# Gate projections of the RG-LRU: one block-diagonal 128x128 product, or four 64x64 products in quarters of the array

## The chip, the cores and the metric

One core of a Trainium2 chip runs the whole program. The metric is the device time of one execution in microseconds, as a median over timed runs. A profiled execution of the same program gives the trace from which all rows below are taken.

## The reference, cut to what matters

Two layers of a decoder trunk run over 2048 tokens of width 1024. The even layer holds retention and stick-breaking attention, the odd layer an HGRN2 recurrence and an RG-LRU. The change touches the gates of the RG-LRU, where each of 8 blocks of 64 channels has its own 64x64 weight for the recurrence gate `r` and for the input gate `ig`:

```
xb = x.reshape(B, S, LRU_BLOCKS, LRU_BW)          # 8 blocks of 64 channels
r  = sigmoid(einsum('bsni,nij->bsnj', xb, w_a).reshape(B, S, W) + b_a)
ig = sigmoid(einsum('bsni,nij->bsnj', xb, w_x).reshape(B, S, W) + b_x)
log_a = -8 * r * softplus(-lam);  a = exp(log_a)
u = sqrt(-expm1(2 * log_a)) * ig * x
h_t = a_t * h_(t-1) + u_t
```

## The kernel before, in words

Everything is float32. Each layer is done in two halves of 1024 tokens, each half in groups `g` of 512 tokens. Activations lie with channels on partitions, so a projection (`proj`, L153) is a stream of 24 products of 128x128 by 128x512 that add into one bank of PSUM, tag `pp`. Its weights and inputs are split in a high and a low part, hence three products for each of 8 blocks of input channels.

The odd layer's half is `hgrn`. It first runs the input projections of HGRN head 0 and of the first 128 channels of the RG-LRU, then weaves the chunk scan of head h (`head_scan`, L829 to L913) with the projections of head h+1 and of RG-LRU channels j = h+1. The scan's products go to PSUM banks of tag `z`, of which there are two; the L880 and L872 products are steps of it. L872 already uses parts of the array: outputs of 32 or 64 partitions, with all 128 input rows.

`lx_proj(j)` handles channels j*128 to j*128+127, two blocks of the RG-LRU. When its two groups are projected, VectorE makes the convolution `xc` (L725 to L727), and `gates(0)` and `gates(1)` are put off through `later` by estimated amounts of TensorE time (L750, L751). A call of `gates(g)` does two float32 products, one for `r` and one for `ig`, each with a block-diagonal 128x128 weight `bd` (L733), and after each product one Sigmoid on ScalarE out of the `z` bank (L734). `gates(1)` goes on with Exp, Tanh and Sqrt (L738 to L740), which need other activation tables than one another in part, and with the scan over time on VectorE (L747), whose result `lg_proj` uses much later. There are 2 halves x 4 j x 2 g = 16 calls.

`bd` is cleared on VectorE (L707) and then filled by four DMAs on the SP queue (L710). The biases `bga` and `bgx` are small constants loaded once by `odd_const` (L701, L702).

The tile framework fixes the order of instructions on each engine when the program is built. It goes by its own estimates of durations: a product that would wait for a bank or an operand by that estimate lets later ready work pass it. A bank of a tag is given to its next user when the last reader of the last user is through.

Of the kernel before, what the change touches and what calls it, by code (L numbers as in the profile page):

```python
# [9 lines left out]
F32 = mybir.dt.float32  # L10
F32R = mybir.dt.float32r
U8 = mybir.dt.uint8
AF = mybir.ActivationFunctionType
# [18 lines left out]
def tile_trunk(ctx: ExitStack, tc: tile.TileContext, a: dict, out: bass.AP):  # L32
    nc = tc.nc
# [4 lines left out]
    const = ctx.enter_context(tc.tile_pool(name="const", bufs=1))  # L38
# [9 lines left out]
    def bank(tag):  # L48
        return (o_bank[-1] if tag == "o" else ps_p).tile([128, 512], F32, tag=tag, name=tag)
# [110 lines left out]
    def later(ns, fn):  # L160
        late.append([ns, fn])
# [47 lines left out]
    def mix_store(half, e, g, t, eng=nc.sync):  # L209
        eng.dma_start(out=mixd[half][g][:, e, :], in_=t)  # L210
# [443 lines left out]
    lam8 = const.tile([128, 4], F32, name="lam8")  # L654
    cw = const.tile([128, 4, 4], F32, name="cw")
    cb = const.tile([128, 4], F32, name="cb")
    bga = const.tile([128, 4], F32, name="bga")
    bgx = const.tile([128, 4], F32, name="bgx")

    def odd_const():  # L660
        with tc.tile_pool(name="oc", bufs=1) as p:
            def ld(name, ap):
                t = p.tile([128, 4], F32, tag=name, name=name)
                nc.sync.dma_start(out=t, in_=ap.rearrange("(j p) -> p j", p=128))
                return t

            lg = ld("lg", a["hgrn_lb_logits"][0])
            t = p.tile([128, 4], F32, name="t")
            e = p.tile([128, 4], F32, name="e")
            nc.vector.tensor_tensor(out=t, in0=lg, in1=lg, op=ALU.subtract)  # L670
            nc.scalar.activation(out=e, in_=t, func=AF.Exp)
            nc.vector.reciprocal(out=t, in_=e)
            nc.vector.tensor_tensor(out=e, in0=e, in1=t, op=ALU.mult)
            nc.vector.tensor_tensor(out=lb, in0=e, in1=e, op=ALU.subtract)
            nc.vector.tensor_scalar(out=olb, in0=lb, scalar1=-1.0, scalar2=1.0, op0=ALU.mult, op1=ALU.add)
            lm = ld("lm", a["lru_lambda"][0])
            ng = p.tile([128, 4], F32, name="ng")
            nc.vector.tensor_scalar(out=ng, in0=lm, scalar1=-1.0, scalar2=None, op0=ALU.mult)
            ab = p.tile([128, 4], F32, name="ab")
            nc.vector.tensor_tensor(out=ab, in0=ng, in1=lm, op=ALU.max)  # L680
            w = p.tile([128, 4], F32, name="w")
            nc.scalar.activation(out=w, in_=ab, func=AF.Exp, scale=-1.0)
            d = p.tile([128, 4], F32, name="d")
            nc.vector.tensor_scalar(out=d, in0=w, scalar1=2.0, scalar2=None, op0=ALU.add)
            nc.vector.reciprocal(out=d, in_=d)
            nc.vector.tensor_tensor(out=w, in0=w, in1=d, op=ALU.mult)
            w2 = p.tile([128, 4], F32, name="w2")
            nc.vector.tensor_tensor(out=w2, in0=w, in1=w, op=ALU.mult)
            s = p.tile([128, 4], F32, name="s")
            nc.vector.memset(s, 1.0 / 19.0)  # L690
            for m in range(17, 0, -2):
                nc.vector.tensor_tensor(out=s, in0=s, in1=w2, op=ALU.mult)
                nc.vector.tensor_scalar(out=s, in0=s, scalar1=1.0 / m, scalar2=None, op0=ALU.add)
            nc.vector.tensor_tensor(out=s, in0=s, in1=w, op=ALU.mult)
            nc.vector.tensor_scalar(out=ng, in0=ng, scalar1=0.0, scalar2=None, op0=ALU.max)
            nc.vector.scalar_tensor_tensor(out=s, in0=s, scalar=2.0, in1=ng, op0=ALU.mult, op1=ALU.add)
            nc.vector.tensor_scalar(out=lam4, in0=s, scalar1=4.0, scalar2=None, op0=ALU.mult)
            nc.vector.tensor_scalar(out=lam8, in0=s, scalar1=-8.0, scalar2=None, op0=ALU.mult)
            nc.sync.dma_start(out=cw, in_=a["conv_w"][0].rearrange("k (j p) -> p k j", p=128))
            nc.sync.dma_start(out=cb, in_=a["conv_b"][0].rearrange("(j p) -> p j", p=128))  # L700
            nc.sync.dma_start(out=bga, in_=a["lru_b_a"][0].rearrange("(j p) -> p j", p=128))  # L701
            nc.sync.dma_start(out=bgx, in_=a["lru_b_x"][0].rearrange("(j p) -> p j", p=128))  # L702

    def lru(half, xT, p1, p5, gt_p, sg_p, M):
        p = p1
        bd = p1.tile([128, 4, 2, 128], F32, name="bd")
        nc.vector.memset(bd, 0.0)  # L707
        for i, nm in enumerate(("lru_w_a", "lru_w_x")):
            for b in range(2):
                nc.sync.dma_start(out=bd[64 * b:64 * b + 64, :, i, 64 * b:64 * b + 64],  # L710
                                  in_=a[nm][0].rearrange("(j b) i o -> b i j o", b=2)[b])
        HT = {}

        def lx_proj(j):
            new = lambda tag: p.tile([128, 1024], F32, tag=tag, name=tag)
            lx = p.tile([128, 1028], F32, tag="lx", name="lx")

            def use_x(g, ps):
                nc.scalar.copy(out=lx[:, 3 + g * 512:515 + g * 512], in_=ps)
                if g == 0:  # L720
                    nc.gpsimd.tensor_copy(out=lx[:, 0:3], in_=lru_x[:, j, :])
                    return
                nc.gpsimd.tensor_copy(out=lru_x[:, j, :], in_=lx[:, 1024:1027])
                xc, r, ig = new("xc"), new("r"), new("ig")
                nc.vector.tensor_scalar(out=xc, in0=lx[:, 0:1024], scalar1=cw[:, 0, j:j + 1], scalar2=cb[:, j:j + 1], op0=ALU.mult, op1=ALU.add)  # L725
                for k in range(1, 4):
                    nc.vector.scalar_tensor_tensor(out=xc, in0=lx[:, k:k + 1024], scalar=cw[:, k, j:j + 1], in1=xc, op0=ALU.mult, op1=ALU.add)  # L727

                def gates(g):
                    c = slice(g * 512, g * 512 + 512)  # L730
                    for i, (t, bias) in enumerate(((r, bga), (ig, bgx))):
                        gp = bank("z")
                        nc.tensor.matmul(gp, bd[:, j, i, :], xc[:, c], start=True, stop=True)  # L733
                        nc.scalar.activation(out=t[:, c], in_=gp, func=AF.Sigmoid, bias=bias[:, j:j + 1])  # L734
                    if g == 0:
                        return
                    av = lx[:, 0:1024]
                    nc.scalar.activation(out=av, in_=r, func=AF.Exp, scale=lam8[:, j:j + 1])  # L738
                    nc.scalar.activation(out=r, in_=r, func=AF.Tanh, scale=lam4[:, j:j + 1])
                    nc.scalar.activation(out=r, in_=r, func=AF.Sqrt)  # L740
                    nc.gpsimd.tensor_tensor(out=ig, in0=ig, in1=xc, op=ALU.mult)
                    nc.vector.scalar_tensor_tensor(out=r, in0=av, scalar=1.0, in1=r, op0=ALU.add, op1=ALU.mult)
                    if half == 0:
                        nc.vector.memset(r[:, 0:1], 1.0)
                    nc.vector.tensor_tensor(out=ig, in0=ig, in1=r, op=ALU.mult)
                    ht = p5.tile([128, 1024], F32, tag="ht", name="ht")
                    nc.vector.tensor_tensor_scan(out=ht, data0=av, data1=ig, initial=lru_h[:, j:j + 1], op0=ALU.mult, op1=ALU.add)  # L747
                    nc.gpsimd.tensor_copy(out=lru_h[:, j:j + 1], in_=ht[:, 1023:1024])
                    HT[j] = ht
                later(6000, lambda: gates(0))  # L750
                later(8000, lambda: gates(1))  # L751

            yield from proj(1, 2048 + j * 128, xT, use_x)

        def lg_proj(j):
            def use_g(g, ps):
                if j == 3 and g == 1:
                    for tt in range(EARLY[1]):
                        mix_rows(half, M, tt, wr_p, "raw")
                gt = gt_p.tile([128, 512], F32, tag="gt", name="gt")  # L760
                silu_to(gt, ps, sg_p)
                last = j == 3
                (nc.vector if last else nc.gpsimd).tensor_tensor(out=gt, in0=gt, in1=HT[j][:, g * 512:g * 512 + 512], op=ALU.mult)
                if last:
                    mix_direct(M, g, gt)
                else:
                    mix_store(half, 4 + j, g, gt)

            yield from proj(1, 2560 + j * 128, xT, use_g)

        return lx_proj, lg_proj
# [225 lines left out]
```

## Time and profile before

| What | Value |
|---|---|
| Time, median of 3 runs | 2305.8 us (2302.98 to 2307.48) |
| Profiled execution, its own time | 2313.08 us |
| Its span, first to last instruction | 2311.2 us |
| TensorE busy | 2233.0 us, 97% of the span |
| VectorE, ScalarE, GpSimd busy | 61%, 48%, 30% |
| Granted TensorE clock, mean | 0.996 of full speed |

The profiled execution lies 7.3 us above the median of the timed runs. TensorE shows two rows: PE for products and PEld for weight loads, which overlap. A float32 product shows as two MATMUL instructions, so 32 gate products are 64 MATMUL rows. A row of the timeline merges instructions that follow without a gap: start, length, engine, line, operation, tiles, shapes, count.

### The profile page before, as it was taken

How to read it: one execution, taken by the hardware profiler on the slowest of the kernel's cores; microseconds unless marked ns; L12 is line 12 of the kernel's file. 1: busy time of each engine (PE TensorE's matmuls, PEld its weight loads, DVE VectorE, ACT ScalarE, POOL GpSimd, SP SyncE). 2: the span in 40 equal slices, each digit the busy share in tenths (PEclk: the TensorE clock that was granted, in tenths of full speed). 3: DMA queues.
4: the chain of work that ended last, by engine and by line, in shares of the span. 5: the costliest groups of instructions: out<-in, count | busy, mean ns of one | idle time of the engine just before them, and what ended most of it. 6: DMA issues, size and time to landing. Idle time of an engine off the chain costs nothing.

```text
span 2311.2 us, 34986 instructions
## 1 busy us (share of the span) xinstructions
PE 2233.0 (97%) x12928; PEld 1886.8 (82%) x12928; DVE 1398.7 (61%) x2113; ACT 1107.5 (48%) x2306; POOL 696.6 (30%) x988
## 2 busy tenths in 40 slices
PE   7999999999999999999899999999999999999998
PEld 6888787789888888787777997878878977878788
DVE  4554666673677776878788454655555535455543
ACT  5443445553466666777666433244245323433431
POOL 0432334410055444555653001222230013122400
PEclk9999999999999999999999999999999999999999
DMA  6333333254622231322223541111126411111161
GB/s 193 110 105 108 106 117 105 92 157 141 209 81 76 82 90 53 94 60 87 81 60 114 184 164 37 42 44 35 49 76 206 163 46 33 46 33 41 64 206 74
DMA packets 244139, 223.11 MB, mean 97 GB/s; under 512 B 21376, under 2 KB 197888, under 8 KB 243968
## 3 DMA queue, kind: packets, MB, share of 16 engines
q1 hardware_dynamic: 243808, 220.35, 31.0%
q8 instruction: 102, 1.67, 0.3%
q14 instruction: 69, 0.57, 0.1%
q0 software_dynamic: 160, 0.52, 0.1%
HBM read 147.43 MB, written 52.43 MB: 86 GB/s over the span
## 4 chain that ended last, share of the span: by engine, by line
PE 76%; DVE 10%; DMA 4%; ACT 4%; issue 3%; POOL 2%; SPq 0%; DVEq 0%; POOLq 0%; ACTq 0%
PE pp L153 42%; PE o L515 4%; PE z L626 4%; PE tr L500 4%; PE pp L626 4%; PE o L626 4%; DVE a L487 2%; PE z L474 2%; PE z L473 2%; DMA mr<-mixd 2%; PE z L880 2%; PE z L733 1%; DVE wtl L505 1%; DVE xc L727 1%; PE tr L113 1%
## 5 line engine op out<-in xcount | busy, mean ns | idle before, releaser
L153 PE MATMUL pp<-xh,wh 128*128 128x512 f32 x1664 | 688.9, 414 | 6.8 <-DVE rst L357 6.2
L153 PE MATMUL pp<-xh,wl 128*128 128x512 f32 x1664 | 658.4, 396 | 2.3 <-DVE wl L133 2.3
L153 PE MATMUL pp<-xl,wh 128*128 128x512 f32 x1664 | 655.8, 394 | 0.0
L153 PEld LDWEIGHTS pp<-xh,wl 128*128 128x128 f32 x1664 | 313.3, 188 | 71.7 <-DVE wl L133 3.5
L490 POOL TENSOR_TENSOR b<-b,a 128x511 f32<-128x511 f32 (+2 forms) x320 | 315.7, 987 | 181.8 <-DVE a L487 109.2
L153 PEld LDWEIGHTS pp<-xh,wh 128*128 128x128 f32 x1664 | 314.5, 189 | 60.3 <-issue 3.0
L153 PEld LDWEIGHTS pp<-xl,wh 128*128 128x128 f32 x1664 | 315.1, 189 | 48.7 <-issue 0.5
L487 DVE TENSOR_TENSOR_SCAN a<-a,past 128x512 f32<-128x512 f32 x192 | 244.4, 1274 | 75.1 <-ACT a L477 74.3
L477 ACT ACTIVATE a<-z 128x512 f32<-128x512 f32 (+2 forms) x320 | 172.2, 538 | 235.6 <-PE z L474 193.5
L133 DVE TENSOR_TENSOR wl<-raw,wh 128x1024 fp32r<-128x1024 f32 x136 | 170.9, 1257 | 128.9 <-ACT wh L132 128.9
L132 ACT CAST wh<-raw 128x1024 fp32r<-128x1024 f32 x136 | 142.9, 1052 | 186.0 <-PE pp L153 159.8
L505 DVE TENSOR_TENSOR wtl<-tr,wth 128x512 fp32r<-128x512 f32 (+1 forms) x320 | 190.3, 596 | 46.5 <-ACT wth L504 45.5
L72 POOL TENSOR_TENSOR rs<-rs,mhalf 128x1 f32<-128x1 f32 (+1 forms) x96 | 67.0, 698 | 479.0 <-DVE rs L71 468.4
L504 ACT CAST wth<-tr 128x512 fp32r<-128x512 f32 (+1 forms) x320 | 169.8, 531 | 72.2 <-PE tr L500 70.6
L500 PE MATMUL tr<-ident,b 128*128 128x128 f32 x1088 | 175.9, 276 | 10.6 <-DVE wtl L505 9.8
L500 PEld LDWEIGHTS tr<-ident,b 128*128 128x128 f32 x1088 | 133.8, 141 | 58.3 <-DVE wtl L505 17.1
L478 ACT ACTIVATE b<-z 128x512 f32<-128x512 f32 (+2 forms) x320 | 171.1, 535 | 0.1
L482 DVE TENSOR_TENSOR_SCAN a<-a,past 128x128 f32<-128x128 f32 (+3 forms) x128 | 104.3, 816 | 91.2 <-ACT a L477 90.6
L515 PE MATMUL o<-wth,v 128*128 128x512 f32 (+1 forms) x320 | 126.8, 396 | 1.1 <-ACT mol L521 1.1
L852 POOL TENSOR_TENSOR kg<-kg,t 128x256 f32<-128x256 f32 x96 | 71.3, 743 | 172.9 <-PE z L880 107.6
L480 POOL TENSOR_SCALAR_AFFINE_SELECT b<-b 128x128 f32<-128x128 f32 x128 | 42.3, 330 | 261.9 <-ACT b L478 223.6
L473 PE MATMUL z<-k,qh 128*128 128x512 f32 (+2 forms) x320 | 119.3, 373 | 1.1 <-DMA qh<-qrh 0.9
(216 smaller groups left out, 4196.7 us busy)
## 6 DMA issues: line engine op xcount, KB each, us to landing
raw<-in_even_w_in SPq DMA_DIRECT2D x56, 512.0 KB, 3.9
raw<-in_odd_w_in SPq DMA_DIRECT2D x48, 512.0 KB, 3.7
xr<-in_x SPq DMA_DIRECT2D x32, 512.0 KB, 5.4
xr<-x1d SPq DMA_DIRECT2D x32, 512.0 KB, 5.3
mr<-mixd SPq DMA_DIRECT2D x32, 448.0 KB, 4.8
qh<-qrh SPq DMA_DIRECT2D x64, 128.0 KB, 2.3
ql<-qrl SPq DMA_DIRECT2D x64, 128.0 KB, 2.4
x1d<-y SPq DMA_DIRECT2D x16, 512.0 KB, 3.5
```

Source lines behind the costliest of these rows:

```text
L133: nc.vector.tensor_tensor(out=wl, in0=raw, in1=wh.bitcast(F32), op=ALU.subtract)
L153: nc.tensor.matmul(ps, w[:, k, :], xx[g][:, k, :], start=(n == 0), stop=(n == 3 * KD - 1))
L473: nc.tensor.matmul(z[:, 0:n], qh[:, tcol], K[e, c][:, 0:n], start=True, stop=False)
L477: nc.scalar.activation(out=A[:, 0:n], in_=z[:, 0:n], func=AF.Sigmoid, scale=-0.125)
L478: nc.scalar.activation(out=B[:, 0:n], in_=z[:, 0:n], func=AF.Sigmoid, scale=0.125)
L487: nc.vector.tensor_tensor_scan(out=A[:, ::-1], data0=A[:, ::-1], data1=past[:, 0:1].to_broadcast([128, 512]), initial=carry[ti][:, 0:1], o ...
L490: nc.gpsimd.tensor_tensor(out=B[:, 0:n - 1], in0=B[:, 0:n - 1], in1=A[:, 1:n], op=ALU.mult)
L500: nc.tensor.transpose(tr[:, ti * 128:ti * 128 + 128], bt[ti][:, sj * 128:sj * 128 + 128], ident)
L504: nc.scalar.copy(out=wh[:, cols], in_=tr[:, cols])
L505: nc.vector.tensor_tensor(out=wl[:, cols], in0=tr[:, cols], in1=wh[:, cols].bitcast(F32), op=ALU.subtract)
L515: nc.tensor.matmul(O[:, cols], V[e, c][:, sj, :], w[:, cols], start=(diag and sj == 0 and w is wh), stop=(c == 0 and sj == 3 and w is wl))
L626: nc.tensor.matmul(ps, m[g][:, k, o:o + 128], w[:, k % 4, :], start=(n == 0), stop=(n == 3 * KD - 1))
```

## The change

The four 64x64 weights of a channel group j are kept without their zero blocks. A product now uses 64 input rows and 64 output columns: input rows of block b, output partitions 64i to 64i+63 with i = 0 for `r` and 1 for `ig`. So both gates of block b share one bank, and the four products of a call lie in four different quarters of the array and two banks. Each Sigmoid reads 64 partitions, so a call has four of them. The memset of `bd` goes, `bd` is half as large, and the two bias tiles become one with the layout that the new outputs want.

```diff
-    bga = const.tile([128, 4], F32, name="bga")
-    bgx = const.tile([128, 4], F32, name="bgx")
+    bg = const.tile([128, 4, 2], F32, name="bg")
...
-            nc.sync.dma_start(out=bga, in_=a["lru_b_a"][0].rearrange("(j p) -> p j", p=128))
-            nc.sync.dma_start(out=bgx, in_=a["lru_b_x"][0].rearrange("(j p) -> p j", p=128))
+            for i, nm in enumerate(("lru_b_a", "lru_b_x")):
+                nc.sync.dma_start(out=bg[64 * i:64 * i + 64], in_=a[nm][0].rearrange("(j b o) -> o j b", b=2, o=64))
...
-        bd = p1.tile([128, 4, 2, 128], F32, name="bd")
-        nc.vector.memset(bd, 0.0)
+        bd = p1.tile([128, 4, 2, 64], F32, name="bd")
         for i, nm in enumerate(("lru_w_a", "lru_w_x")):
             for b in range(2):
-                nc.sync.dma_start(out=bd[64 * b:64 * b + 64, :, i, 64 * b:64 * b + 64],
+                nc.sync.dma_start(out=bd[64 * b:64 * b + 64, :, i, :],
                                   in_=a[nm][0].rearrange("(j b) i o -> b i j o", b=2)[b])
...
-                    for i, (t, bias) in enumerate(((r, bga), (ig, bgx))):
-                        gp = bank("z")
-                        nc.tensor.matmul(gp, bd[:, j, i, :], xc[:, c], start=True, stop=True)
-                        nc.scalar.activation(out=t[:, c], in_=gp, func=AF.Sigmoid, bias=bias[:, j:j + 1])
+                    gp = [bank("z") for b in range(2)]
+                    h = [slice(64 * b, 64 * b + 64) for b in range(2)]
+                    for i in range(2):
+                        for b in range(2):
+                            nc.tensor.matmul(gp[b][h[i], :], bd[h[b], j, i, :], xc[h[b], c], start=True, stop=True)
+                    for i, t in enumerate((r, ig)):
+                        for b in range(2):
+                            nc.scalar.activation(out=t[h[b], c], in_=gp[b][h[i], :], func=AF.Sigmoid, bias=bg[h[i], j, b:b + 1])
```

## Rows read from the trace of the kernel before

**Rows 1.** The page: span, busy time by engine, the last chain by line.

```profile
span 2311.2 us, 34986 instructions
...
PE 2233.0 (97%) x12928; PEld 1886.8 (82%) x12928; DVE 1398.7 (61%) x2113; ACT 1107.5 (48%) x2306; POOL 696.6 (30%) x988
...
PE pp L153 42%; PE o L515 4%; PE z L626 4%; PE tr L500 4%; PE pp L626 4%; PE o L626 4%; DVE a L487 2%; PE z L474 2%; PE z L473 2%; DMA mr<-mixd 2%; PE z L880 2%; PE z L733 1%; DVE wtl L505 1%; DVE xc L727 1%; PE tr L113 1%
```

**Rows 2.** A weave window: PE, PEld, DVE, ACT, POOL busy (count), PEclk, DMA.

```profile
1513.00:1592.00 79.00, 78.66 (x439) 63.86 (x438) 44.17 (x76) 30.20 (x56) 20.23 (x24) 1.00 0.13 40
```

**Rows 3.** Gate products, line L733: ns min/median/max; then one cause of idle before.

```profile
L733 PE MATMUL z<-xc,bd x64: 590/592/697, 1430.7 to 2150.0; 128*128 128x512 f32 x64
...
  ACT r L734: 1.5, 2
```

**Rows 4.** TensorE's timeline: two calls back to back; one call and its follower.

```profile
1430.73 3.89 PE L733 MATMUL z<-xc,bd 128*128 128x512 f32 x8
...
1516.69 1.88 PE L733 MATMUL z<-xc,bd 128*128 128x512 f32 x4
1518.54 0.63 PE L880 MATMUL z<-qf,kg 128*128 128x64 f32 x4
```

**Rows 5.** L872, 32-column burst, in growing windows: products begun (x) by each end.

```profile
1485.00:1485.14 0.14, 0.01 (x1) 0.01 (x1) 1.00 0.43 117
1485.00:1485.27 0.27, 0.14 (x4) 0.14 (x5) 1.00 0.22 61
1485.00:1485.38 0.38, 0.25 (x11) 0.25 (x12) 1.00 0.16 43
1485.00:1485.54 0.54, 0.41 (x16) 0.41 (x16) 1.00 0.11 30
```

**Rows 6.** TensorE's timeline around an L872 burst in 64-column tiles.

```profile
1487.60 0.39 PE L153 MATMUL pp<-xh,wl 128*128 128x512 f32 x1
1487.92 0.68 PE L872 MATMUL z<-qf,kg 128*64 128x64 f32 x8
1488.53 0.50 PE L153 MATMUL pp<-xh,wh 128*128 128x512 f32 x1
1488.86 0.39 PE L153 MATMUL pp<-xl,wh 128*128 128x512 f32 x1
```

**Rows 7.** TensorE's timeline around a gate call between projection products.

```profile
1674.94 0.39 PE L153 MATMUL pp<-xh,wh 128*128 128x512 f32 x1
1675.17 1.88 PE L733 MATMUL z<-xc,bd 128*128 128x512 f32 x4
1676.49 0.79 PE L153 MATMUL pp<-xl,wh 128*128 128x512 f32 x1
1677.12 0.39 PE L153 MATMUL pp<-xh,wl 128*128 128x512 f32 x1
```

**Rows 8.** ScalarE's timeline after the call of 1516.69.

```profile
1517.76 0.69 ACT L734 ACTIVATE r<-z,bga 128x512 f32<-128x512 f32 x1 [1.10 <-PE z L733]
1518.46 1.28 ACT L738 ACT_TABLE_LOAD   x1
...
1522.22 0.69 ACT L734 ACTIVATE ig<-z,bgx 128x512 f32<-128x512 f32 x1
```

**Rows 9.** ScalarE groups in 1430 to 1725: busy us, mean ns, idle before.

```profile
L860 ACT COPY m<-qf 128x256 f32<-128x256 f32 x8 | 3.4, 423 | 4.6 <-PE z L841 4.3
...
L875 ACT COPY at<-z 64x256 f32<-64x256 f32 x8 | 2.9, 365 | 12.0 <-PE z L872 12.0
```

**Rows 10.** What TensorE waited for in 1430 to 1725, the largest: us, times, longest.

```profile
PE z L880 <- POOL kg L852: 1.8, 5, 0.7
```

**Rows 11.** The memset of bd; what SP waited for there; a bias load.

```profile
L707 DVE MEMSET bd<- x2: 912/912/912, 1335.8 to 1808.5; 128x1024 f32 x2
...
SPq L710 <- DVE bd L707: 19.6, 1, 19.6
...
25.80 0.51 SPq L701 DMA_DIRECT2D bga<-in_lru_b_a  x1
```

## The prediction

> **What bounds the kernel now.** I read the page first [rows 1]. TensorE is busy for 2233.0 of 2311.2 us, and the chain that ended last is a list of TensorE lines; the gates' L733 has 1% of it. An average over the span decides nothing, so I then cut the odd layer into windows. In one weave of scan and projections TensorE is busy for 78.66 of 79.00 us, ScalarE for 30.20 and VectorE for 44.17 [rows 2]. The list of what TensorE waited for there has as its largest entry 1.8 us in 300 us [rows 10]. So in the stage that holds the gates, a microsecond of TensorE saved is a microsecond of the end, and a microsecond more on another engine costs nothing unless TensorE comes to wait for it. The clock is 1.00 of full speed, the 2.4 GHz level, in that window [rows 2]. Then I read the gates' own lines, what they wait for, and who waits for them.
>
> **What a gate call costs TensorE.** A call is four MATMUL rows, two for each float32 product. From the merged row, (1.88 - 0.59) / 3 = 0.43 us from start to start [rows 3, 4]. A call therefore takes 4 x 0.43 = 1.71 us, and the 16 calls 27.4 us. Going there and back costs nothing: from the projection product before to the second one after is 2.18 us [rows 7], and 1.71 plus two projection products of 0.23 is 2.17.
>
> **Removed and added on TensorE.** After the change a call has eight MATMUL rows of 64x64 by 512 columns. Each still streams 512 columns, so I price each at 0.43 us. Everything hangs on how many run side by side. Bounds: all four quarters together, 2 x 0.43 = 0.85 us a call, which saves 0.85 x 16 = 13.7 us; all after one another, 8 x 0.43 = 3.42 us, which costs 27.4 us. Row tiles do not occur in the trace, but column tiles do. The L872 burst in 32-column tiles sends eight MATMULs to one column range and then eight to another. By the windows, 3 begin in the first 0.13 us, then 7 in 0.11 us, then 5 in up to 0.16 us [rows 5]. The outer stretches show what one range alone does, some 30 to 45 ns apiece; the middle is twice as dense, so both ranges run at once. I take full overlap because this is the nearest row, and keep half and none for the range.
>
> A tile that has its second half-product still queued does not hold up another tile either. At the 32 ns apiece of the last stretch, the eighth MATMUL of the first range begins about 1485.37, yet eleven have begun by 1485.38 [rows 5]: the second range started while the first still had work in line. That matters here, because each quarter gets its two MATMULs directly behind one another. The Trainium skill says otherwise ("TensorE: Matmul & The Clock Gate", Part 3): products start and end in strict program order. By that rule a quarter's second MATMUL would hold back the next quarter's first, so five steps of 0.43 us and not two would make a call; that is rival C below, and the trace speaks against it.
>
> **Changing the shape of the array.** The L872 burst in 64-column tiles shows a price that the gates did not pay. From the product before to the second after is 1.26 us [rows 6]. Its eight MATMULs of 64 columns are worth 8 x 0.43 / 8 = 0.43 us, the two projection products 0.46, so 0.37 us goes into changing over and back. Of the 16 calls, two stand directly behind another one (the merged eight of [rows 4], and one like it in the second half), so there are 14 excursions: 14 x 0.37 = 5.2 us. Starting four quarters one after the other adds something: nothing at least, 0.1 us a call at most by some 30 ns for each start [rows 5]; I take 0.06, so 1.0 us. TensorE's net so far: -13.7 + 5.2 + 1.0 = -7.5 us.
>
> **ScalarE and the z banks.** A Sigmoid of 512 columns took 0.69 us [rows 8]. With half the partitions it will take as long: 64x256 took 365 ns, 128x256 423 ns, the first out of PSUM [rows 9]. So a call has 4 x 0.69 instead of 2 x 0.69, in total 32 x 0.69 = 22 us more of ScalarE, which has about 49 of 79 us free [rows 2]. It is not free for the banks. Before, the r bank returned when the first Sigmoid ended, 1518.45, 1.76 us after the call began, and the next scan product started at 1518.54, 0.1 us later, just as TensorE came free [rows 4, 8]. Now a bank holds r and ig of one block, so it returns after the third and the fourth Sigmoid. The first Sigmoid cannot begin before about 1.2 us (one MATMUL step of 0.43, some 0.1 for starts, 0.59 for the last, and the 0.05 by which 1517.76 lies behind 1516.69 + 0.43 + 0.59); the third ends at 1.2 + 3 x 0.70 = 3.3 us, the fourth at 4.0 us. TensorE is done with the call at about 1.3 us, changeovers included. If the next z product stood directly behind, TensorE would wait 3.4 - 1.3 = 2.1 us where it waited next to nothing before. Nine projection products (9 x 0.23) between them cover it, and the framework's order puts work there that does not need the bank, as far as its estimate of times is right. Evidence that it is mostly right: in all calls together TensorE waited for a reader of r for 1.5 us, in 2 places [rows 3], although ig's bank stayed taken until 1522.9 in this call [rows 8]. Bounds: 0 and 2.1 us a call; I take 0.25, near the low end, because that row shows waits of this sort well covered, so 4.0 us in all. Behind a waiting z product on TensorE's queue stands everything, since it runs in order.
>
> The skill has a rule against this change here ("TensorEngine Tiling (Array Packing)", PSUM Bottleneck): packing speeds up TensorE but not the emptying of PSUM, which may then be the limit. That is rival B, and the sum by it stands there.
>
> **The rest.** The memset, 0.91 us twice on VectorE, goes [rows 11]; VectorE is not the limit. The SP queue sat 19.6 us before L710 until the memset was through [rows 11], and what stands behind it are stores and loads that follow other work; now the loads of `bd` wait for the buffer alone, at the same place. I cost this at nothing: the weights are used some 90 us later (the memset at 1335.8, L733 first at 1430.73 [rows 4, 11]). If that cover went, a late weight would cost its landing, a few us, once a half. The bias loads stay two, with as many single elements, issued around 25.80, long before use [rows 11]. Exp, Tanh, Sqrt and the scan over time start about 1.4 us later in a call; their result is wanted by projections many us later.
>
> **Sum.** -13.7 + 5.2 + 1.0 + 4.0 = -3.5 us. The profiled execution took 2313.1 us, so its like would take 2309.6. It stands 7.3 us above the median of 2305.8; the same difference from the median gives 2302.3 us, say 2302. With no waits for banks it is 2298.3; at 0.5 us a call 2306.3.
>
> **The rivals.** A change of 0.2%, 4.6 us, is about what a measurement of this kernel can tell from none.
>
> A. The sum above: full overlap, bank waits mostly covered, 2298 to 2306. For it: [rows 5], [rows 3]. Chance 0.44; about half of that lies below 2301.2, half within 0.2%.
>
> B. Full overlap, but TensorE waits for the z banks. If the order counts on four products one after another, it expects TensorE to need 3.4 us for a call and places the next z product for when the third Sigmoid then ends: the third product's end at 2.6 us, and three Sigmoids, of which the second waits for the fourth product, put that at 4.8. It would leave 1.4 us of other work; TensorE would in truth be done after 1.3, reach the z product at 2.7 and wait 0.7 us, and longer where a second call follows at once. At 0.9 a call: -7.5 + 14.4 = +6.9, 2313 us. It decides for slower from (7.5 + 4.6) / 16 = 0.76 us a call on, and ends the gain at 0.47. Against it: the small waits before [rows 3]. Chance 0.26, of which 0.10 within 0.2%.
>
> C. Overlap by half or less than half. Two at a time gives back nothing: 0 + 5.2 + 1.0 + 2 for waits = +8, 2314 us, chance 0.12. If a quarter's second MATMUL holds back the next quarter's first, the seconds of one overlap only the firsts of the next: five steps of 0.43 against four before, 0.43 x 16 = 6.9, with 5.2 and 1.0 makes +13, 2319 us, chance 0.08. Against it: [rows 5]; for it: that row shows columns only, never rows. Together 0.20, nearly all slower.
>
> D. No overlap: the change does not do what it says. +27.4 + 5.2 = +32.6, 2338 us. Against it: [rows 5]. Chance 0.10, slower.
>
> **How the numbers follow.** Case A is the likeliest, so 2302 is the time; its own range is 2298 to 2306. Faster by over 0.2%: 0.22 from A, and 0.08 more for an order of instructions that happens to fall better than counted, 0.30. Within 0.2%: 0.20 from A, 0.10 from B, 0.02 from C, together 0.32. Slower: the rest of B, C and D, 0.38 after the shift to the first. The range runs from 2296, the no-wait sum less 2 us for a lucky order, to 2321, which holds B and C with the strict order, and leaves out D and little else.
>
> **What would show it.** Right: MATMUL rows of a call begin within about 0.2 us of each other in four and again after 0.43 us, a call's eight within about 1.2 us; excursions cost 0.37 us more than before; the four Sigmoids take 0.69 us each, in the order r, r, ig, ig. TensorE's waits for ScalarE L734's successor lines total a few us. Wrong: MATMUL rows of different quarters 0.43 us apart (C or D), or waits of z products (L880, L841, the second call) for those Sigmoids of 10 us or more (B). The prediction also fails if the new order of TensorE's work opens waits far from the gates, at the stage's end above all.

## The result and the profile after

The changed kernel takes 2320.5 us (median of 5 runs, 2314.12 to 2324.61), the kernel before 2305.8 us (5 runs). The ratio is 1.006, 95% interval 1.0044 to 1.0076: slower by about 14 us, where 2302 was forecast. First the span and the busy line from the page of the profiled execution, then the weave window that is the counterpart of [rows 2]:

```profile
span 2318.5 us, 35135 instructions
...
PE 2231.8 (96%) x12992; PEld 1879.2 (81%) x12992; DVE 1399.2 (60%) x2111; ACT 1119.2 (48%) x2330; POOL 699.3 (30%) x988
```

```profile
1513.00:1592.00 79.00, 76.62 (x434) 61.68 (x432) 43.39 (x74) 30.78 (x58) 20.61 (x24) 1.00 0.14 40
```

TensorE's sum of busy time has hardly moved, but in the window it stands idle for 2.38 us where it was idle for 0.34 [rows 2]. From the last product of one output projection (L626) to the first of the next, the odd layer's stage grew from 369.6 and 370.6 us in the two halves to 376.3 and 377.3: 13.4 of the lost microseconds lie there. (The two profiled spans differ by 7.3 us only, because the profiled execution of the kernel before lies 7.3 us above its median.) The gates' own line, of all 16 calls, as in [rows 3]:

```profile
L733 PE MATMUL z<-xc,bd x128: 589/600/641, 1427.5 to 2156.8; 64*64 64x512 f32 x128
...
  ACT ig L736: 5.3, 12
```

There are twice the MATMUL rows, of the same length, and 5.3 us of waits in 12 places for the Sigmoids of `ig`. These 5.3 us are idle time of the weight loader (PEld): the row of the products shows none of it, because one quarter at work counts as busy. TensorE's timeline around the two calls of one `j` (the counterpart of [rows 4, 7]):

```profile
1510.27 0.39 PE L153 MATMUL pp<-xl,wh 128*128 128x512 f32 x1
1510.81 1.33 PE L733 MATMUL z<-xc,bd 64*64 64x512 f32 x8 [0.16 <-DVE xc L725]
1512.07 0.50 PE L153 MATMUL pp<-xh,wl 128*128 128x512 f32 x1
...
1514.01 0.40 PE L153 MATMUL pp<-xh,wl 128*128 128x512 f32 x1
1514.34 1.76 PE L733 MATMUL z<-xc,bd 64*64 64x512 f32 x8
1516.03 0.50 PE L153 MATMUL pp<-xh,wh 128*128 128x512 f32 x1
```

The first call takes 1.26 us up to the next product, the second 1.69, as much as a call before (1.71 by the prediction's sum). ScalarE shows why. Its timeline (the counterpart of [rows 8]):

```profile
1513.57 1.39 ACT L736 ACTIVATE ig<-z,bg 64x512 f32<-64x512 f32 x2
1514.99 0.58 ACT L803 COPY vt<-tr 128x512 f32<-128x512 f32 x1
1516.14 1.39 ACT L736 ACTIVATE r<-z,bg 64x512 f32<-64x512 f32 x2 [0.57 <-PE z L733]
1517.56 1.39 ACT L736 ACTIVATE ig<-z,bg 64x512 f32<-64x512 f32 x2
1518.96 1.28 ACT L740 ACT_TABLE_LOAD   x1
```

The first call's two banks come back when the two `ig` Sigmoids end, about 1514.26 and 1514.96. The second call's first quarter starts at 1514.34; the first one in the second bank starts at 1515.02. The other quarter of the first bank stands behind it in the code and starts together with it, though its own bank was free. Summed over the calls, late banks cost some 5 us (measured below), and that does not make 13.4. The larger part is in the list of what TensorE waited for in 1430 to 1725 (the counterpart of [rows 10], which had 1.8 us as its largest):

```profile
PE z L882 <- POOL kg L854: 5.2, 7, 1.4
PE tr L888 <- POOL kg L854: 1.6, 1, 1.6
PE z L874 <- POOL kg L854: 1.4, 1, 1.4
```

L854 is the scan's step on GpSimd that multiplies `kg` (L852 before), L882 and L874 the scan products that read it (L880 and L872 before). In the whole span these waits are 9.9, 2.1 and 2.7 us, against 4.2 at L880 and 0.7 at L886 before. One of them, on GpSimd's timeline and then on TensorE's:

```profile
1519.02 2.39 POOL L743 TENSOR_TENSOR ig<-ig,xc 128x1024 f32<-128x1024 f32 x1 [9.44 <-ACT ig L736]
1521.37 0.82 POOL L854 TENSOR_TENSOR kg<-kg,t 128x256 f32<-128x256 f32 x1
```

```profile
1517.97 0.39 PE L153 MATMUL pp<-xh,wl 128*128 128x512 f32 x1
1518.34 1.08 PE L882 MATMUL z<-qf,kg 128*128 128x64 f32 x8
...
1520.46 0.40 PE L153 MATMUL pp<-xh,wl 128*128 128x512 f32 x1
1522.25 1.10 PE L882 MATMUL z<-qf,kg 128*128 128x64 f32 x8 [1.39 <-POOL kg L854]
```

GpSimd sits idle until `ig` is there, does the product `ig*xc` for 2.39 us, and only then the `kg` step, in the order that the framework has given its queue. The step overwrites what the scan product at 1518.34 reads, and that product was through by 1519.4. TensorE's own order has six projection products before the next scan product, and then it waits 1.39 us. The same place in the kernel before, GpSimd's timeline:

```profile
1523.80 0.63 POOL L852 TENSOR_TENSOR kg<-kg,t 128x256 f32<-128x256 f32 x1 [3.38 <-PE z L880]
1524.38 2.57 POOL L741 TENSOR_TENSOR ig<-ig,xc 128x1024 f32<-128x1024 f32 x1
1527.14 0.80 POOL L852 TENSOR_TENSOR kg<-kg,t 128x256 f32<-128x256 f32 x1 [0.18 <-PE z L872]
```

There the product stood behind a `kg` step and was through when the next was due. In the trace after, six of the eight `ig*xc` (all but j = 0) are followed by a TensorE wait of 1.37 to 1.39 us: 8.3 us. Two of the six are followed by a stretch at the lower clock level; windows around one that ended at 1998.76:

```profile
1997.00:2000.50 3.50, 2.11 (x14) 1.61 (x13) 1.81 (x3) 2.56 (x3) 2.19 (x3) 1.00 0.00 0
2000.50:2003.90 3.40, 3.40 (x25) 2.58 (x24) 0.85 (x2) 1.12 (x2) 0.94 (x2) 0.50 0.03 7
2003.90:2010.00 6.10, 6.10 (x34) 4.80 (x33) 4.58 (x5) 4.14 (x8) 1.27 (x2) 1.00 0.00 0
```

In such a stretch (1.2 GHz) one projection product begins 0.43 us after another, against 0.23 us at the full clock, so the two stretches of 3.4 us cost some 3.2 us (an estimate from these steps). The kernel before has such stretches too, but none in this stage.

### The profile page after: what moved, and what is told of

The parts are those of the page before. It is cut to its first block, busy times and chain, and to the rows that moved or that the text cites. A ratio compares the mean times of both kernels' runs of the same rounds, so it can differ in the third digit from the quotient of the medians.

```text
span 2318.5 us, 35135 instructions
## 1 busy us (share of the span) xinstructions
PE 2231.8 (96%) x12992; PEld 1879.2 (81%) x12992; DVE 1399.2 (60%) x2111; ACT 1119.2 (48%) x2330; POOL 699.3 (30%) x988
## 3 DMA queue, kind: packets, MB, share of 16 engines
q8 instruction: 103, 1.69, 0.3%
## 4 chain that ended last, share of the span: by engine, by line
PE 76%; DVE 10%; ACT 4%; DMA 4%; issue 3%; POOL 3%; SPq 0%; DVEq 0%; POOLq 0%; ACTq 0%
PE pp L153 41%; PE z L626 4%; PE pp L626 4%; PE o L515 4%; PE tr L500 4%; PE o L626 4%; DVE a L487 2%; PE z L474 2%; PE z L473 2%; PE z L882 2%; DMA mr<-mixd 2%; DVE wtl L505 1%; DVE xc L725 1%; POOL kg L854 1%; PE z L733 1%
## 5 line engine op out<-in xcount | busy, mean ns | idle before, releaser
L515 PE MATMUL o<-wtl,v 128*128 128x512 f32 (+1 forms) x320 | 118.0, 369 | 0.0
```

The source lines that it names most:

```text
L515: nc.tensor.matmul(O[:, cols], V[e, c][:, sj, :], w[:, cols], start=(diag and sj == 0 and w is wh), stop=(c == 0 and sj == 3 and w is wl))
```

## The experiments

Two theories stood against each other. **Banks**: the loss is the two `z` banks held by both gates, with the split second calls. **GpSimd order**: the loss is `ig*xc` ahead of the `kg` step. A third was that each needs the other. The expectations call the banks rival Z, the order on GpSimd theory P, and the third theory B+P; rival M is the price of changing the array's shape. `tr` and `o` are the tags of two more pairs of PSUM banks, used for transposes and for the scan's output. The runs in one table (ratio to the kernel before on the same chip; `kg` waits are all rows of TensorE's list of waits that name the `kg` step, summed over the span; the kernel before has 4.9):

| Kernel | Median us | Ratio (95%) | `kg` waits, us |
|---|---|---|---|
| changed, again | 2321.98 | 1.0072 (1.0058 to 1.0086) | 14.7 |
| tr bank, product ahead | 2319.29 | 1.0062 (1.0046 to 1.0077) | 16.2 |
| product one step later | 2315.38 | 1.0046 (1.0032 to 1.0060) | 10.9 |
| layout alone, full products | 2311.76 | 1.0020 (1.0011 to 1.0028) | 4.3 |
| before, `ig` first | 2307.79 | 1.0003 (0.9991 to 1.0014) | 5.9 |
| product on VectorE | 2307.25 | 0.9998 (0.9989 to 1.0007) | 7.4 |
| before, product on VectorE | 2305.30 | 1.0000 (0.9991 to 1.0009) | 3.8 |
| diagonal, calls together | 2302.54 | 0.9978 (0.9969 to 0.9987) | 2.5 |
| tr bank | 2301.11 | 0.9969 (0.9956 to 0.9981) | 4.2 |
| tr bank, product on VectorE | 2300.81 | 0.9974 (0.9966 to 0.9983) | 5.2 |
| diagonal | 2299.06 | 0.9966 (0.9954 to 0.9978) | 2.5 |
| diagonal, o and tr banks | 2295.64 | 0.9958 (0.9943 to 0.9973) | 4.2 |

**The product off GpSimd.** In the changed kernel, and as a control in the kernel before:

```diff
-                    nc.gpsimd.tensor_tensor(out=ig, in0=ig, in1=xc, op=ALU.mult)
+                    nc.vector.tensor_tensor(out=ig, in0=ig, in1=xc, op=ALU.mult)
```

> The changed kernel, with the product ig*xc (L743, 2.39 us) on VectorE instead of GpSimd, so that no scan step of GpSimd (L854, kg) stands behind it. Theory P (TensorE's new waits, some 5 us a half, come from kg steps queued behind L743): the 1.38 us waits of TensorE for kg go, its idle time in the odd layer falls by 8 us or more over both halves, and the time by 6 to 10 us against the changed kernel, to a ratio of 1.001 to 1.004 to the kernel before. Rival Z (waits for the z banks, in and behind a call) and rival M (changing the array's shape): no change, ratio 1.006.

> A control: the kernel before, with ig*xc on VectorE. If theory P is right, that product stood in nobody's way before, and the ratio is 0.998 to 1.002. If the move is a gain by itself, as the rival has it, the ratio is 0.993 to 0.996.

The whole loss is gone in the changed kernel (0.9998), more than the 6 to 10 us that theory P expected, and the same edit does nothing for the kernel before (1.0000), so it is no gain of its own. The gate calls are as split as they were: from a call's first product to the next other product, all 16 take 22.9 us in both. TensorE's waits for the `kg` step, in the span:

```profile
PE z L882 <- POOL kg L854: 4.3, 10, 0.7
PE tr L888 <- POOL kg L854: 2.8, 4, 1.6
PE z L874 <- POOL kg L854: 0.3, 1, 0.3
```

The 1.4 us waits of L882 and L874 are gone; the 1.6 us at L888 has stayed.

**Parts of the change alone.** Two products of 128x128 for each call, with the changed kernel's outputs (both gates of a block in one bank, four Sigmoids). The weights get their zero blocks and the memset back; those lines are cut here:

```diff
...
-                    for i in range(2):
-                        for b in range(2):
-                            nc.tensor.matmul(gp[b][h[i], :], bd[h[b], j, i, :], xc[h[b], c], start=True, stop=True)
+                    for b in range(2):
+                        nc.tensor.matmul(gp[b], bd[:, j, b, :], xc[:, c], start=True, stop=True)
```

> The layout of the outputs without the quarters: two full 128x128 products a call, one for each block of 64 channels, with r in the upper and ig in the lower partitions of its bank, zeros in the weights for the other block, and the four Sigmoids of 64 partitions as in the changed kernel. TensorE pays 1.71 us a call as before and no change of the array's shape. Theory P: the early ig puts L743 ahead of a kg step as in the changed kernel, the long waits for kg stay, and it is slower than before by 8 us or more, ratio 1.004 to 1.008. Rival M: no slower than before, ratio 0.998 to 1.002. Rival Z: slower, by the bank waits alone, with z products that wait for L736 of 0.5 us a call or more.

Slower by 4.6 us (2.5 to 6.5): more Sigmoids and longer held banks cost something without any quarters, about a third of the loss. `ig*xc` stands behind a `kg` step here at j = 1 to 3, as before, so theory P's condition did not come about and this run says nothing on it. And the kernel before with Exp held back behind the `ig` Sigmoid, so that `ig` is early:

```diff
-                        nc.scalar.activation(out=t[:, c], in_=gp, func=AF.Sigmoid, bias=bias[:, j:j + 1])
+                        sig = nc.scalar.activation(out=t[:, c], in_=gp, func=AF.Sigmoid, bias=bias[:, j:j + 1])
...
-                    nc.scalar.activation(out=av, in_=r, func=AF.Exp, scale=lam8[:, j:j + 1])
+                    with tc.issue_after(sig.ins):
+                        nc.scalar.activation(out=av, in_=r, func=AF.Exp, scale=lam8[:, j:j + 1])
```

> The kernel before, with Exp made to stand behind the second call's ig Sigmoid on ScalarE. Products, banks and array stay as before. ig is then ready some 4 us earlier and its bank returns earlier, one table load of 1.28 us goes in each of 8 places, but GpSimd gets its 2.4 us product earlier too. Theory P: waits of TensorE for kg behind that product appear in the kernel before as well and it is slower by 4 to 10 us, ratio 1.002 to 1.004. Rivals Z and M: the same or faster, ratio 0.997 to 1.000.

No change, where theory P expected 1.002 to 1.004: an early `ig` alone costs nothing that can be measured. In its trace the product at j = 1 and 2 again starts directly behind a `kg` step (at 1512.39, in line behind one); at j = 3 it got ahead of one, with waits of 0.6 us.

**Banks and order, two by two.** First another bank for the second block, which leaves one `z` bank to the scan:

```diff
-                    gp = [bank("z") for b in range(2)]
+                    gp = [bank("z"), bank("tr")]
```

> The changed kernel with the second block's products in a bank of tag tr, which has two of its own, so that a call takes one z bank and not both. Theory P: the second call of a pair no longer splits (its eight MATMULs begin within 0.6 us, as in the first call), which saves 8 x 0.4 = 3 us; the waits for kg go only where L743 stands at another place in GpSimd's order. Ratio 1.003 to 1.006. Rival Z: most of the loss goes, ratio 1.000 or less.

Faster by 7 us (4.4 to 10.1): theory P's forecast missed, and rival Z's held. The call of the same `j` on TensorE's timeline, where the two tags keep the rows apart:

```profile
1507.97 0.39 PE L153 MATMUL pp<-xl,wh 128*128 128x512 f32 x1
1508.52 0.61 PE L733 MATMUL z<-xc,bd 64*64 64x512 f32 x1 [0.16 <-DVE xc L725]
1508.53 0.64 PE L733 MATMUL tr<-xc,bd 64*64 64x512 f32 x1
...
1508.54 0.64 PE L733 MATMUL tr<-xc,bd 64*64 64x512 f32 x1
1508.97 0.59 PE L733 MATMUL z<-xc,bd 64*64 64x512 f32 x1
...
1509.02 0.59 PE L733 MATMUL tr<-xc,bd 64*64 64x512 f32 x1
1509.54 0.50 PE L153 MATMUL pp<-xh,wl 128*128 128x512 f32 x1
1509.88 0.40 PE L153 MATMUL pp<-xh,wh 128*128 128x512 f32 x1
```

Four quarters begin within 0.02 us, again 0.45 later, and the next other product begins 1.02 us after the first. All 16 calls take 17.9 us by that measure. One call in each half, the second at j = 3, still begins in two parts, 0.6 us apart, for a bank that VectorE gave back late. But GpSimd's order changed with the bank:

```profile
1513.04 0.65 POOL L854 TENSOR_TENSOR kg<-kg,t 128x256 f32<-128x256 f32 x1 [5.75 <-PE z L882]
1515.34 2.38 POOL L743 TENSOR_TENSOR ig<-ig,xc 128x1024 f32<-128x1024 f32 x1 [1.65 <-ACT ig L736]
1517.68 0.81 POOL L854 TENSOR_TENSOR kg<-kg,t 128x256 f32<-128x256 f32 x1
```

With a `z` bank free, the scan product comes before the Sigmoids are through, its `kg` step 2.3 us before `ig`, and the product meets nobody. So this run alone can't tell the theories apart. Two more runs cross them: the changed kernel with the product and what follows it (`tail`, whose body is cut here) put behind the next `kg` step, and the tr kernel with the `kg` step held behind the product.

```diff
+                    tails.append([2, tail])
...
+                    for item in list(tails):
+                        item[0] -= 1
+                        if item[0] <= 0:
+                            tails.remove(item)
+                            with tc.issue_after(kg_step.ins):
+                                item[1]()
```

> The changed kernel with one swap on GpSimd's queue in each of the 8 places: ig*xc (L743) now stands behind the scan step (kg) that it stood ahead of. Orders of ScalarE and VectorE are the same, TensorE's in all but a few rows. Theory P: the waits of 1.38 us for kg behind the second call go, TensorE's idle time in the odd layer falls by 8 us or more, and the time falls by as much as with the product on VectorE, to a ratio of 0.999 to 1.002. Rival, that VectorE's faster product or GpSimd's lower load did it there: ratio 1.004 to 1.006.

```diff
-                    nc.gpsimd.tensor_tensor(out=ig, in0=ig, in1=xc, op=ALU.mult)
+                    muls.append([2, nc.gpsimd.tensor_tensor(out=ig, in0=ig, in1=xc, op=ALU.mult)])
...
+                    with tc.issue_after(due[0][1].ins) if due else nullcontext():
+                        nc.gpsimd.tensor_tensor(out=kv[:, :, 0, :], in0=kv[:, :, 0, :], in1=bc(1), op=ALU.mult)
```

> The kernel with the tr bank (ratio 0.9969), with the one swap on GpSimd's queue turned back: ig*xc ahead of the scan step again, as in the changed kernel; TensorE's order differs in two rows. It makes the fourth of four: bank z or tr, ig*xc ahead or behind. Theory B+P (the late banks and the product on GpSimd cost only together, since the bank's return and ig's readiness then fall together): no long waits for kg, ratio 0.996 to 0.999. Theory P alone: slower than with the product behind by 5 us or more, ratio 0.999 or above.

The second is the clean one. With the tr bank, and gate calls as short as in the faster kernel (17.9 us), the order alone turns 0.9969 into 1.0062, a swing of some 21 us. Its list of waits, in the span:

```profile
PE z L889 <- POOL kg L861: 11.5, 14, 2.3
...
PE z L881 <- POOL kg L861: 3.1, 2, 1.6
PE tr L895 <- POOL kg L861: 1.6, 2, 0.9
```

Four of its six waits behind the product are 2.25 us, and three of these four are followed by a stretch of 3.4 us at half clock; the profiled execution is the slowest of six (2327.32 us). The forced order makes these waits longer than the changed kernel's 1.39 us, so the 21 us are not its price there. But the order costs with either bank, and the theory that it needs the split falls.

The first, the other corner, recovers only a part (1.0046), where theory P expected 0.999 to 1.002; it lies in the band of the rival, that VectorE's faster product or GpSimd's lower load had done it. Its trace has the two collisions of j = 1 and 2 gone in each half, but new ones at j = 0 and a step later at j = 3, again waits of 1.35 to 1.43 us: four where there were six, and 10.9 us of `kg` waits between the 14.7 and 7.4 of its neighbours in the table. It is not a corner without collisions, so the two by two isn't complete, and this run by itself does not exclude that rival; that moving the product does nothing for the kernel before, and the order alone so much for the tr kernel, speak against it.

> The changed kernel itself, beside the others on one chip, so that the four of bank and order can be compared: ratio 1.005 to 1.007. If the swap behind the kg step alone was worth something, it lies above that one's 1.0046 by 0.001 or more.

The changed kernel run again beside them gave 1.0072. Its trace has the same six waits (1.36 to 1.40 us), but only one of them is followed by a stretch at half clock.

**The other cross.** The tr bank and the product on VectorE together:

> The changed kernel with the second block's bank from tag tr and with ig*xc on VectorE, both at once. If the bank of tag tr took away the queue's collision as well as the split of the second call, the two do not add up: ratio 0.995 to 0.998, as with the bank alone (0.9969). If the collision is still there with the bank, another 4 us or more go: ratio 0.995 or less.

0.9974, as with the bank alone. Beside the run with the product on VectorE and two `z` banks (0.9998), where nothing in the code differs but the bank, this prices the two `z` banks: 0.0024 x 2306 = 5.5 us, with some 3 us of error either way. The framework's order changes with the bank, and the `kg` waits fall from 7.4 to 5.2 us, so not all of it need be bank waits.

**A version that gains.** `r` of both blocks in the diagonal quarters and one bank, so one Sigmoid over 128 partitions does it; `ig` in the other two quarters, in a tr bank, with two Sigmoids (shown against the changed kernel; the biases, in two tiles again, are cut):

```diff
-                    gp = [bank("z") for b in range(2)]
+                    gp = [bank("z"), bank("tr")]
...
-                            nc.tensor.matmul(gp[b][h[i], :], bd[h[b], j, i, :], xc[h[b], c], start=True, stop=True)
+                            nc.tensor.matmul(gp[i][h[b ^ i], :], bd[h[b], j, i, :], xc[h[b], c], start=True, stop=True)
-                    for i, t in enumerate((r, ig)):
-                        for b in range(2):
-                            nc.scalar.activation(out=t[h[b], c], in_=gp[b][h[i], :], func=AF.Sigmoid, bias=bg[h[i], j, b:b + 1])
+                    nc.scalar.activation(out=r[:, c], in_=gp[0], func=AF.Sigmoid, bias=bga[:, j:j + 1])
+                    for b in range(2):
+                        nc.scalar.activation(out=ig[h[b], c], in_=gp[1][h[1 - b], :], func=AF.Sigmoid, bias=bgx[h[1 - b], j:j + 1])
```

> The quarters placed otherwise: r's two products in the diagonal quarters, so that r fills one z bank in channel order and one Sigmoid of 128 partitions empties it; ig's two in the other quarters and a tr bank, with two Sigmoids. Three Sigmoids a call instead of four, and the z bank returns after the first. If what is left of the cost with the tr bank is the z bank's return or ScalarE, it is faster than that by 2 us or more, ratio 0.994 to 0.996; if not, 0.996 to 0.998. Two row tiles write one bank in different partitions here; if they do not overlap then, a call takes 1.7 us or more and the ratio is 0.999 or above.

Two quarters with different input rows now write the same bank, on different partitions, and still run side by side:

```profile
1509.57 0.65 PE L735 MATMUL z<-xc,bd 64*64 64x512 f32 x2 [0.16 <-DVE xc L727]
1509.59 0.65 PE L735 MATMUL tr<-xc,bd 64*64 64x512 f32 x2
1510.02 0.62 PE L735 MATMUL z<-xc,bd 64*64 64x512 f32 x2
1510.07 0.59 PE L735 MATMUL tr<-xc,bd 64*64 64x512 f32 x2
```

Calls take 16.2 us in all; the 1.7 us less than with the tr bank is what the second calls there lost to late banks, in them and at the scan product behind. The time is 0.9966, a gain on the kernel before but no clear step from the tr kernel's 0.9969. Two ways on from it: the first call put off until the second (`later(8000)` for 6000), and no `z` bank at all (`bank("o")` for `bank("z")`).

> Diagonal quarters with z and tr, and both calls of a channel group put off to the same moment, so that they follow each other directly: 8 excursions into quarters instead of 14. If an excursion costs 0.37 us, the gate calls and what stands around them save 6 x 0.37 = 2.2 us where the banks allow it (each tag has two banks, so the second call finds one of each): ratio 0.995 to 0.996. If the second call waits for the first one's banks, or its later work comes too late, nothing is won: 0.997 or more.

> Diagonal quarters for r, the others for ig (three Sigmoids), with r's bank from tag o and ig's from tag tr, so that a call holds no z bank at all. If what is left of the cost lies in the z bank that r still held, TensorE's idle time falls by 2 us or more and the ratio goes to 0.995 or less; if the two tags only move the wait to transposes and the scan's output, it stays at 0.996 to 0.998.

Together the calls win nothing (0.9978, not clearly worse than 0.9966): most pairs do run as one (1510.20 to 1512.11 for both), which saves a changeover, but at j = 3 the pair is cut by the banks: its first call's products begin from 1664.48 to 1667.01. Without a `z` bank the time is the lowest of all, 2295.64 us, 0.9958 (0.9943 to 0.9973), 10 us below the kernel before; it lies between the two forecasts and is not clear of the 0.9966. This is so though at j = 0 the product got ahead of a `kg` step again, with a wait of 1.25 us in each half.

## Why the prediction was wrong, point by point

**The array: right.** Four quarters overlap fully. An excursion runs from the product before a call to the second product after it. For the first call at j = 1 it is 1509.88 - 1507.97 = 1.91 us in the tr kernel. The same call in the kernel before, with the same wait for `xc`, took 1516.00 - 1513.43 = 2.57:

```profile
1513.43 0.39 PE L153 MATMUL pp<-xl,wh 128*128 128x512 f32 x1
1513.97 1.96 PE L733 MATMUL z<-xc,bd 128*128 128x512 f32 x4 [0.16 <-DVE xc L727]
...
1516.00 0.39 PE L153 MATMUL pp<-xh,wh 128*128 128x512 f32 x1
```

Without the wait a call begins 0.33 us after the product before it (1514.01 to 1514.34 in the changed kernel), so an excursion is 0.33 + 1.02 + 0.34 = 1.69 us, an estimate put together from these rows. Against 2.18 [rows 7] that saves 0.49, where the prediction's terms give 0.43: changing over and starting took 0.38 us, not 0.43. Without waits it had TensorE gain 7.5 us; the kernels with a tr bank gained 7 (tr), 8 (diagonal) and 10 (o and tr), net of what else changed in their order. One count was off by a little: the calls that stood back to back before came apart in the changed kernel, so it has 16 excursions and not 14.

A half-product still in line holds no other quarter up either. In the changed kernel's call of 1510.81 the other three quarters' first products begin at 1511.06 and 1511.07, before the first quarter's second one at 1511.26. In its call of 1514.34, the same code, the first quarter's second one begins at 1514.82, before the others' first ones at 1515.02. Windows over both calls, of that line alone (in parentheses the products in flight in each stretch: four first ones; one quarter's two; and then its second with three first ones):

```profile
1511.00:1511.20 0.20, 0.20 (x4) 0.14 (x6) 1.00 0.00 0
1514.60:1515.00 0.40, 0.40 (x2) 0.00 (x0) 1.00 0.00 0
1515.00:1515.20 0.20, 0.20 (x4) 0.18 (x6) 1.00 0.00 0
```

No single order of these products fits both calls (the queue's own order is not in the trace; it is taken to be the same for both, as the code is). So rivals C and D are out. The rule of the Trainium skill ("TensorE: Matmul & The Clock Gate", Part 3) that products start in strict program order does not hold between quarters here.

**The banks: right in size, wrong in place.** The prediction took 4.0 us. The difference of 22.9 and 17.9 us of call time is 5.0, and the pair of runs on VectorE gives 5.5. But little of it lies at a scan product behind a call, which the order covers well (nine projection products stand between 1516.03 and 1518.34). Most of it lies in the second call of a pair, whose second bank is 0.7 us behind its first. The evidence for small waits was misread, too: the 1.5 us of [rows 3] are idle time of the weight loader, as the 5.3 are here. Rival B's mechanism was there at about a third of its 14.4 us. The Trainium skill's warning behind it ("TensorEngine Tiling (Array Packing)", PSUM Bottleneck) agrees with the trace so far. The time came out near the 2319 of rival C, with nothing of C in it, and so inside the stated range, which had been kept that wide for C: that is luck.

**ScalarE: right.** Sigmoids of 64 partitions take 0.69 us, in the order r, r, ig, ig.

**The rest, at nothing: the step that failed.** The prediction said that another engine's microseconds cost nothing unless TensorE comes to wait for it, and that Exp, Tanh, Sqrt and the scan over time come 1.4 us later, with their result wanted many us later. It followed the values to their use and not the queue on which they are made. GpSimd is busy for 30%, but `ig*xc` blocks it for 2.4 us, and the scan's `kg` step, on which TensorE waits, is behind it. And `ig` is not later but earlier. Before, Exp and two table loads stood between `r` and `ig`, so `ig` was ready 5.15 us after the `r` Sigmoid began (1517.76 to 1522.91, [rows 8]); after, 2.8 us (1516.14 to 1518.95), since all four Sigmoids hold ScalarE until the banks are read. At the same time the two `z` banks held the scan product off until 1518.34, so that its `kg` step became ready at about the same time as `ig`, and the framework put the product first. What came is the prediction's last sign of being wrong, waits far from the gates, but by the order on GpSimd and not on TensorE.

By the runs this step is worth 14 to 17 us: the difference between the changed kernel (1.006 and 1.0072) and the same with the product on VectorE (0.9998). One change of tag cured both the bank waits and the order; that fits a common cause, two `z` banks held at once.

**The account.** Of the stage's +13.4 us in the profile, gate calls give -4.4, TensorE's idle time +10.7 (waits for `kg` +9.8 of it), the slower clock some +3.2. Some 3.9 us are not booked. In the kernel with the product on VectorE a like rest of 2.8 is left, with one `z` bank 0.1 (tr), 0.3 (tr and VectorE) and 1.5 (diagonal), with none 0.0; so most of it seems to go with the two `z` banks. Part of it can be seen: a projection product counts as busy for 0.39 us while the next usually begins after 0.23, so a wait of up to 0.16 us leaves no idle time. In that way ten L882 products begin 0.08 to 0.16 us late, 1.3 us in all (one is at 1518.34, 0.37 us behind the product of 1517.97); the kernel before has none, the kernel on VectorE ten, the tr kernel two.

**What stays open.** Why the clock fell after some of the six waits (two in one profiled execution, one in the other) and not after the others was not tried. A corner with two `z` banks and no collision on GpSimd was not reached.

## What to carry to other kernels

When a change makes a value ready earlier or later, look at what stands behind its consumer on that engine's queue, whose order is fixed when the program is built, even if the engine is busy for 30% only. Here that cost 1.4 us of waiting a time, and in all about twice what the change was to save on TensorE. Packing products into quarters of the array pays only as fast as banks return, so give the parts banks that come back independently of the ones that the critical chain uses, and let one read empty a bank where the layout allows it. A profile in which every engine but one is idle most of the time does not say that the order on those engines is free.

## What the runs showed of the hardware

Four 64x64 float32 products in their own quarters begin within 0.02 us and run side by side in full: eight MATMULs of 512 columns take 1.02 us up to the next product. With the way in and out that is 1.69 us (estimated from rows, see above), against 2.18 us for four of 128x128. Two quarters with different input rows that write different partitions of one bank do so as well (starts within 0.02 us, 1.02 us a call). A quarter's second MATMUL still in line did not hold up another quarter's first. Soon after a wait of TensorE, busy until then, the granted clock fell to 0.50 (1.2 GHz) for 3.4 us in some places: after two of six waits of 1.37 to 1.39 us in the changed kernel (one of six in its second profiled execution), and after three of four of 2.25 us in the tr kernel with the product ahead.
